# Forty first halves ahead of the expert stage, its first gates loaded in pieces, and a new table of durations for the list scheduler

## The chip, the core and the metric

One NeuronCore of a Trainium2 chip runs the whole program in one launch. The metric is the device time of one execution in microseconds (us), median of the runs given. The engines are TensorE (PE; PEld is its weight load), VectorE (DVE), ScalarE (ACT), GpSimd (POOL) and SyncE (SP). Loads and stores are issued by SP, ACT and POOL and carried by 16 DMA engines.

## The reference, cut to what matters

Two blocks run one after the other on 512 tokens of 1024 channels, in float32: a conformer convolution beside an RWKV-7 recurrence, then a sparse attention, then a convolution and pooling mixer, and at the end a layer of small experts (PEER) and a gated projection. The change is about the expert layer:

```python
def peer_block(xb, w_q, sub_keys, expert_u, expert_v):
    q = (xb @ w_q).reshape(T, 8, 2, 128)
    s = jnp.einsum('thpd,hpkd->thpk', q, sub_keys)       # 128 keys, twice
    sv, si = lax.top_k(s, 16)
    ...                                                   # best 16 of the 16 x 16 sums
    gate = jax.nn.softmax(top_s.astype(jnp.float32), axis=-1)
    u = jnp.take(expert_u, eidx, axis=0)                  # 128 x 128 experts, one row each
    act = jax.nn.gelu(jnp.einsum('thkd,td->thk', u, xb))
    v = jnp.take(expert_v, eidx, axis=0)
    return jnp.einsum('thk,thkd->td', gate * act, v)
```

## The kernel before, in words

The expert layer is done in two ways at once. For 352 of the 512 tokens (TD) it is dense: the 16,384 experts are cut into 128 groups of 128 rows, called experts e below. The first half of e is gelu(U_e x), 24 matmuls of 352 columns; the second half multiplies it by the gates of e, splits it and multiplies it by V_e, 24 more matmuls. Every float32 product is three float32r products of a high and a low part, so each weight tile is split: `wh` on ACT (L207) and `wl` on POOL (L209), in pieces of 256 columns, four for a first half. For the other 160 tokens, rows of U and V are gathered by index (L1338, POOL queue, 512 KB each, 320 of them) and multiplied and summed on DVE (L1353, L1369).

`route` finds the chosen experts and turns them into gates: for each token a one-hot product (L1519 and L1522 on DVE, L1527 on ACT, L1528 on POOL, L1533 on PE, L1536 on ACT) written to `gs` in DRAM by 11 stores of 2 MB, one for 32 tokens (L1537, SP). I call this the one-hot stage. Some first halves need no gate, and NS = 32 of them are done beside `route`: the list `early` takes every fourth e and then, if NS is larger, e = 1, 9, 17 and so on. The gelu of such an expert is stored to `ga` in DRAM (L1208, ACT queue) and loaded back later (L1230, ACT queue). After each one GE gathered rows may be pulled, and after each expert of the last stage GR.

When `route` and the 32 are done, its tile pools close, and the pool `vp` of the last stage opens on the same memory. `prep` runs over experts by threes (GV): for each fourth e it loads the gates of four experts from `gs` into `g4` (L1227, ACT queue, one transfer of 704 KB, two buffers), takes the gelu from `ga` or makes it (`u_phase`, L1199), multiplies it by its gates (L1234), splits it (L241, L242), loads V_e (`vraw`, L1241, SP queue) and splits that too (L1244 on ACT, L1248 on POOL, a quarter at L1246 on DVE). The second halves of three experts follow (L1264 to L1266, sums at L1268). I call this the expert stage.

The order of all instructions on each engine is not that of the program text. `Order` reads the built program, gives every instruction a duration (`cost`), and lists the instructions by a simulation with priorities (`run`); `best` keeps the shortest of twelve such lists, and `impose` makes it the order of each engine. What `cost` and `run` say decides the order of the whole kernel, and only that. `run` also holds each transfer of SP and ACT until the eighth before it has landed (LANES), and the first instruction of a pool until the pools under it are done (`over`).

Of the kernel before, what the change touches and what calls it, by code (L numbers as in the profile page):

```python
# [133 lines left out]
class Net:  # L134
# [1038 lines left out]

    UQ = 1
    NS = 32
    GV = 3
    GA = 4
    BW = 6
# [2 lines left out]
    def peer(self):  # L1182
        nc, tc, I = self.nc, self.tc, self.I
        self.pair.close()
        self.psum2 = None
        with ExitStack() as L:
# [4 lines left out]
            gs = dr.tile([self.TD // 32, 128, 128, 32], F32, name="gs")  # L1191
# [24 lines left out]
            with ExitStack() as VP:  # L1216
                vp = VP.enter_context(tc.tile_pool(name="vp", bufs=1))
                g4 = None
                GV = self.GV

                def prep(e0):
                    nonlocal g4
                    wh, wl, vh, vl = [], [], [], []
                    for e in range(e0, min(128, e0 + GV)):
                        if e % 4 == 0:
                            g4 = vp.tile([128, self.TD // 32, 4, 32], F32, name="g4", bufs=2)
                            nc.scalar.dma_start(g4, gs[:, :, e:e + 4, :].rearrange("g k e t -> k g e t"))  # L1227
                        if e in early:
                            g = up.tile([128, self.TD], F32, name="ga", bufs=self.GA)
                            nc.scalar.dma_start(g, ga[early.index(e)])  # L1230
                        else:
                            g = u_phase(e, False)
                        gv = g.rearrange("p (g t) -> p g t", t=32)
                        nc.vector.tensor_tensor(gv, gv, g4[:, :, e % 4, :], OP.mult)  # L1234
                        h = vp.tile([128, self.TD], F32R, name="wwh", bufs=self.BW)
                        l = vp.tile([128, self.TD], F32R, name="wwl", bufs=self.BW)
                        self.split(h, l, g)
                        wh.append(h)
                        wl.append(l)
                        raw = vp.tile([128, 1024], F32, name="vraw", bufs=2)  # L1240
                        nc.sync.dma_start(raw, I["ev"][e])  # L1241
                        h = vp.tile([128, 1024], F32R, name="vh", bufs=self.BV)
                        l = vp.tile([128, 1024], F32R, name="vl", bufs=self.BV)
                        nc.scalar.activation(h, raw, AF.Copy)  # L1244
                        if e % 8 in self.VD:
                            nc.vector.tensor_tensor(l, raw, h.bitcast(F32), OP.subtract)  # L1246
                        else:
                            nc.gpsimd.tensor_tensor(l, raw, h.bitcast(F32), OP.subtract)  # L1248
                            self.pool = self.last()
                        self.pull(self.GR)  # L1250
                        vh.append(h)
                        vl.append(l)
                    return wh, wl, vh, vl
# [21 lines left out]
    TB = 32  # L1275
    VD = (1, 5)
    GN = 5
    GE = 2.0
    GR = 2.0

    def gather_open(self, L):
# [285 lines left out]
class Order:  # L1567
# [4 lines left out]
    SETS = {"Exp": (0, 6), "Tanh": (0, 2, 18), "Ln": (5, 6), "Silu": (18,), "Sigmoid": (2,), "Sin": (18,),  # L1572
            "Gelu_apprx_tanh": (11,)}
    LOAD, SWITCH, LANES = 1283, 4000, 8
    TICK, BUSY = 10240 / 3, 3060
    SHAPE = 94

    def __init__(self, nc):
# [15 lines left out]
    def cost(self, i):  # L1594
# [3 lines left out]
        out = list(i.outs)  # L1598
# [4 lines left out]
        def psum(a):  # L1603
            return self.mem.get(a.memref, ("",))[0] == "PSUM"
        if "DMA" in op and e == "Pool":
            return e, 0, 1038, 0, 4 * math.prod(c for _, c in out[0].ap)
        if "DMA" in op:
            run = min(list(a.ap)[-1][1] if list(a.ap)[-1][0] == 1 else 1 for a in ins + out)
            return e, 0, 450 if run >= 128 else 625, 0, 4 * math.prod(c for _, c in out[0].ap) * (1 if run >= 128 else 2)
# [3 lines left out]
        if e == "PE":  # L1613
            n = size(out[0])
            rows, cols = i.tile_size
            self.shape[i.name] = rows, cols
            one = n / 2.4
            self.col[i.name] = n * rows / 128
            if i.tile_position[1]:
                return e, cols / 1.2, 20, 20, 0  # L1620
            p = 2 if i.is_transpose else 1 if str(i.ins[0].dtype).endswith("float32r") and n >= 256 else 4
            self.col[i.name] *= p
            return e, cols / (2.4 if i.is_transpose else 1.2), p * one + 2.5, one, 0
        sc = sum(size(a) == 1 for a in ins) if n > 1 else 0
        big = [a for a in ins if size(a) > 1]
        if e == "Activation":
# [2 lines left out]
        if e == "DVE":  # L1629
            if op == "Memset":  # L1630
                return e, 0, n / 0.96 + 8, 0, 0
            fast = op in ("TensorScalarPtr", "TensorCopy") and len(big) < 2 and not any(map(psum, ins))
            return e, 0, (n / (2 if fast else 1) + 66 + 60 * sc) / 0.96, 0, 0
        if op == "Memset":
            return e, 0, n / 1.2 + 36, 0, 0
        return e, 0, n * (2.1 if len(big) > 1 else 3.3) + 150, 0, 0
# [113 lines left out]
    def run(self, pri):  # L1750
# [19 lines left out]
        soon = {e: [] for e in self.HOP}  # L1770
        now = {e: [] for e in self.HOP}
        lanes, cols, ring, dma, array, table, shape = [], {}, 0.0, 0.0, 0.0, None, None
        out = []

        def push(n):
# [12 lines left out]
        while len(out) < len(self.seq):  # L1788
# [31 lines left out]
                lanes.append(dma)  # L1820
            elif e == "PE":
                k = int(max(array, t) / self.TICK)
                slow = 1 if cols.get(k - 1, 0) >= self.BUSY else 2
                d += self.SHAPE if self.shape[n] != shape else 0
                shape = self.shape[n]
                array = end[n] = max(array, t + load * slow) + d * slow
                free[e] = array - last * slow + 3
                k = int(array / self.TICK)
                cols[k] = cols.get(k, 0) + self.col[n]
            else:  # L1830
                end[n] = t + d
                free[e] = end[n] + 3
# [80 lines left out]
```

## Time and profile before

| | us |
|---|---|
| median of 3 runs | 2848.27 (2845.97 to 2852.17) |
| profiled execution, its time | 2844.42 |
| profiled execution, its span | 2842.7 |
| PE busy in the span | 2609.6 |
| DVE busy in the span | 2154.0 |
| POOL busy in the span | 1724.6 |
| ACT busy in the span | 1481.2 |

The span runs from the first to the last instruction of the profiled execution, and all times of the trace are counted from its start. The time of that execution is 1.7 us longer than its span. The mean clock granted to TensorE was 0.965 of full speed.

### The profile page before, as it was taken

How to read it: one execution, taken by the hardware profiler on the slowest of the kernel's cores; microseconds unless marked ns; L12 is line 12 of the kernel's file. 1: busy time of each engine (PE TensorE's matmuls, PEld its weight loads, DVE VectorE, ACT ScalarE, POOL GpSimd, SP SyncE). 2: the span in 40 equal slices, each digit the busy share in tenths (PEclk: the TensorE clock that was granted, in tenths of full speed). 3: DMA queues.
4: the chain of work that ended last, by engine and by line, in shares of the span. 5: the costliest groups of instructions: out<-in, count | busy, mean ns of one | idle time of the engine just before them, and what ended most of it. 6: DMA issues, size and time to landing. Idle time of an engine off the chain costs nothing. (4 is left out here: it accounts for less than half of the span.)

```text
span 2842.7 us, 45654 instructions
## 1 busy us (share of the span) xinstructions
PE 2609.6 (92%) x14715; PEld 2220.0 (78%) x14715; DVE 2154.0 (76%) x4307; ACT 1481.2 (52%) x3177; POOL 1724.6 (61%) x1870
## 2 busy tenths in 40 slices
PE   5889999999798899999999987779999999999996
PEld 3656667666576688887888777779999999999995
DVE  6686669865379998954669999667877787787875
ACT  6646557568455358965353367424334333344435
POOL 4423523222164443346657788779988888899973
PEclk9889899999899999999999999989999999999998
DMA  8744355555872221223334356889999999999972
GB/s 260 172 96 97 82 117 119 103 145 122 216 241 91 71 80 46 71 84 106 92 111 141 107 193 251 293 299 326 338 321 334 334 337 335 309 334 330 336 253 80
DMA packets 353444, 552.27 MB, mean 194 GB/s; under 512 B 60082, under 2 KB 239154, under 8 KB 351539
## 3 DMA queue, kind: packets, MB, share of 16 engines
q1 hardware_dynamic: 224690, 295.22, 32.2%
q0 software_dynamic: 64800, 201.88, 23.9%
q10 hardware_dynamic: 63712, 52.24, 5.8%
q8 instruction: 116, 1.90, 0.3%
q14 instruction: 126, 1.02, 0.1%
HBM read 507.76 MB, written 41.42 MB: 193 GB/s over the span
## 5 line engine op out<-in xcount | busy, mean ns | idle before, releaser
L209 POOL TENSOR_TENSOR wl<-wraw,wh 128x256 fp32r<-128x256 f32 x937 | 748.3, 816 | 395.8 <-ACT wh L207 314.8
L207 ACT ACTIVATE wh<-wraw 128x256 fp32r<-128x256 f32 x937 | 363.0, 411 | 422.0 <-PE mm L217 198.2
L216 PE MATMUL mm<-xh,wh 128*128 128x352 f32 (+1 forms) x1464 | 513.2, 352 | 32.4 <-ACT wh L207 17.4
L218 PE MATMUL mm<-xh,wl 128*128 128x352 f32 (+1 forms) x1464 | 510.6, 352 | 18.8 <-POOL wl L209 18.8
L217 PE MATMUL mm<-xl,wh 128*128 128x352 f32 (+1 forms) x1464 | 510.5, 350 | 2.3 <-DVE xl L287 2.3
L216 PEld LDWEIGHTS mm<-xh,wh 128*128 128x128 f32 x1464 | 280.5, 192 | 57.2 <-ACT wh L207 21.0
L218 PEld LDWEIGHTS mm<-xh,wl 128*128 128x128 f32 x1464 | 280.5, 192 | 42.1 <-POOL wl L209 24.5
L217 PEld LDWEIGHTS mm<-xl,wh 128*128 128x128 f32 x1464 | 280.8, 192 | 23.3 <-DVE xl L287 4.6
L192 POOL DMA_DIRECT2D dl<-in_wev x114 | 100.7, 904 | 284.1 <-ACT dl L191 261.3
L1248 POOL TENSOR_TENSOR vl<-vraw,vh 128x1024 fp32r<-128x1024 f32 x96 | 230.9, 2407 | 4.0 <-ACT vh L1244 3.0
L1369 DVE SCALAR_TENSOR_TENSOR wide<-grow,gdot,wide 128x1024 f32<-128x1024 f32 x158 | 202.4, 1281 | 17.1 <-DMA grow<-in_ev,gidx 15.9
L218 PE MATMUL mm<-xh,dl 128*128 128x512 f32 x456 | 197.0, 436 | 15.5 <-DMA dl<-in_wev 15.5
L1353 DVE SCALAR_TENSOR_TENSOR gscr<-grow,wide 128x1024 bf16<-128x1024 f32 x160 | 194.1, 1213 | 19.4 <-DMA grow<-in_ue,gidx 18.1
L1199 ACT ACTIVATE mm<-mm 128x352 f32<-128x352 f32 x96 | 43.0, 448 | 314.4 <-PE mm L218 308.5
L216 PE MATMUL mm<-xh,dh 128*128 128x512 f32 x456 | 193.4, 428 | 13.0 <-ACT xh L355 12.3
L1338 POOL DMA_INDIRECT grow<-in_ue,gidx x160 | 164.2, 1026 | 57.8 <-DVE gscr L1353 20.2
L217 PE MATMUL mm<-xl,dh 128*128 128x512 f32 x456 | 191.1, 422 | 6.2 <-DVE xl L356 6.2
L1338 POOL DMA_INDIRECT grow<-in_ev,gidx x160 | 162.6, 1016 | 42.8 <-issue 18.1
L1244 ACT ACTIVATE vh<-vraw 128x1024 fp32r<-128x1024 f32 x128 | 134.4, 1054 | 83.2 <-DMA vraw<-in_ev 70.5
L1264 PE MATMUL xu<-wwh,vh 128*128 128x352 f32 x512 | 167.0, 326 | 5.2 <-DVE x L1268 2.6
L1266 PE MATMUL xu<-wwh,vl 128*128 128x352 f32 x512 | 166.1, 326 | 4.6 <-POOL vl L1248 2.6
L1265 PE MATMUL xu<-wwl,vh 128*128 128x352 f32 x512 | 165.8, 324 | 0.0
(582 smaller groups left out, 6818.7 us busy)
## 6 DMA issues: line engine op xcount, KB each, us to landing
vraw<-in_ev SPq DMA_DIRECT2D x128, 512.0 KB, 5.7
wraw<-in_uT SPq DMA_DIRECT2D x494, 128.0 KB, 4.7
draw<-in_wev SPq DMA_DIRECT2D x114, 256.0 KB, 3.4
dl<-in_wev POOLq DMA_DIRECT2D x114, 256.0 KB, 4.7
gs<-st SPq DMA_DIRECT2D x11, 2048.0 KB, 7.7
g<-gs ACTq DMA_DIRECT2D x32, 704.0 KB, 10.3
wraw<-in_wod SPq DMA_DIRECT2D x156, 128.0 KB, 2.2
adaw<-in_adaT SPq DMA_DIRECT2D x32, 512.0 KB, 8.1
```

What stands on the lines that cost most here:

```text
L207: nc.scalar.activation(wh, raw[:, s], AF.Copy)
L209: nc.gpsimd.tensor_tensor(wl, raw[:, s], wh.bitcast(F32), OP.subtract)
L216: nc.tensor.matmul(ps, wh, xh, start=start, stop=False)
L217: nc.tensor.matmul(ps, wh, xl, start=False, stop=False)
L218: nc.tensor.matmul(ps, wl, xh, start=False, stop=stop)
L1248: nc.gpsimd.tensor_tensor(l, raw, h.bitcast(F32), OP.subtract)
L1264: nc.tensor.matmul(po, vh[i][:, s], wh[i], start=(i == 0), stop=False)
L1265: nc.tensor.matmul(po, vh[i][:, s], wl[i], start=False, stop=False)
L1266: nc.tensor.matmul(po, vl[i][:, s], wh[i], start=False, stop=(i == len(wh) - 1))
L1338: self.nc.gpsimd.indirect_dma_start(out=t, out_offset=None, in_=src, in_offset=bass.IndirectOffsetOnAxis(ap=self.gidx[i][:, k:k + 1], axis=0))
L1353: nc.vector.scalar_tensor_tensor(scr, u, 1.0, x, op0=OP.mult, op1=OP.mult, accum_out=self.gdot[i][:, k:k + 1])
L1369: nc.vector.scalar_tensor_tensor(acc, r, w, acc, op0=OP.mult, op1=OP.add)
```

## The change

`NS` goes from 32 to 40, so that the first halves of e = 1, 9, 17, 25, 33, 41, 49 and 57 are done beside `route` too, and `GE` from 2.0 to 1.6, so that the number of gathered rows pulled there stays 64. The first two gate loads (e = 0 and 4) are issued as 11 transfers of 64 KB each. In `Order` the durations of some operations are changed: a float32r matmul costs 12.5 ns more, DVE operations that read two operands from SBUF (or run in the fast mode) cost a quarter more per element, the accumulating transfer of POOL costs less to issue and more to carry, and the clock of PE is followed window by window: it goes up and down at two different counts of columns.

```diff
@@ -1173,7 +1173,7 @@
     UQ = 1
-    NS = 32
+    NS = 40
     GV = 3
@@ -1224,7 +1224,11 @@
                         if e % 4 == 0:
                             g4 = vp.tile([128, self.TD // 32, 4, 32], F32, name="g4", bufs=2)
-                            nc.scalar.dma_start(g4, gs[:, :, e:e + 4, :].rearrange("g k e t -> k g e t"))
+
+                            for i in range(self.TD // 32 if e < 8 else 0):
+                                nc.scalar.dma_start(g4[:, i], gs[i, :, e:e + 4, :])
+                            if e >= 8:
+                                nc.scalar.dma_start(g4, gs[:, :, e:e + 4, :].rearrange("g k e t -> k g e t"))
@@ -1275,7 +1279,7 @@
     GN = 5
-    GE = 2.0
+    GE = 1.6
     GR = 2.0
@@ -1572,7 +1576,8 @@
     LOAD, SWITCH, LANES = 1283, 4000, 8
-    TICK, BUSY = 10240 / 3, 3060
+    TICK, BUSY, FULL = 10240 / 3, 4000, 7200
+    PORT = 1.25
     SHAPE = 94
@@ -1603,7 +1608,8 @@
         if "DMA" in op and e == "Pool":
-            return e, 0, 1038, 0, 4 * math.prod(c for _, c in out[0].ap)
+            add = str(out[0].dtype).endswith("float32r")
+            return e, 0, 920 if add else 1038, 0, (10 if add else 4) * math.prod(c for _, c in out[0].ap)
@@ -1620,7 +1626,7 @@
             self.col[i.name] *= p
-            return e, cols / (2.4 if i.is_transpose else 1.2), p * one + 2.5, one, 0
+            return e, cols / (2.4 if i.is_transpose else 1.2), p * one + (15 if p == 1 else 2.5), one, 0
@@ -1630,7 +1636,8 @@
             fast = op in ("TensorScalarPtr", "TensorCopy") and len(big) < 2 and not any(map(psum, ins))
-            return e, 0, (n / (2 if fast else 1) + 66 + 60 * sc) / 0.96, 0, 0
+            port = fast or sum(not psum(a) for a in big) > 1
+            return e, 0, (n / (2 if fast else 1) * (self.PORT if port else 1) + 66 + 60 * sc) / 0.96, 0, 0
@@ -1770,6 +1777,7 @@
         lanes, cols, ring, dma, array, table, shape = [], {}, 0.0, 0.0, 0.0, None, None
+        tick, slow = 0, 2
@@ -1820,7 +1828,10 @@
                 k = int(max(array, t) / self.TICK)
-                slow = 1 if cols.get(k - 1, 0) >= self.BUSY else 2
+                while tick < k:
+                    c2 = cols.get(tick, 0)
+                    slow = (1 if c2 >= self.FULL / 2 else 2) if slow == 2 else 2 if c2 < self.BUSY else 1
+                    tick += 1
```

## Rows read from the trace of the kernel before

**Rows 1.** Busy time of each engine by stage (window, its length, then each engine).
```profile
core 0: us, PE busy (x) PEld busy (x) DVE busy (x) ACT busy (x) POOL busy (x), PEclk, DMA share, GB/s
0.00:1482.00 1482.00, 1355.82 (x7186) 1019.13 (x7187) 1074.18 (x2151) 891.21 (x1855) 612.38 (x791) 0.96 0.46 120
1482.00:1658.00 176.00, 163.20 (x866) 145.11 (x865) 174.76 (x887) 67.46 (x163) 130.80 (x160) 0.97 0.42 129
1658.00:1806.00 148.00, 117.74 (x866) 108.15 (x864) 144.74 (x136) 114.12 (x305) 122.65 (x90) 0.99 0.63 230
1806.00:1844.00 38.00, 32.21 (x165) 29.90 (x164) 18.86 (x32) 10.31 (x26) 25.75 (x33) 0.87 0.96 347
1844.00:1873.00 29.00, 9.69 (x37) 8.17 (x37) 10.86 (x16) 6.52 (x15) 16.26 (x17) 0.65 0.86 288
1873.00:2760.00 887.00, 870.81 (x5325) 862.31 (x5324) 685.61 (x1029) 349.37 (x742) 791.20 (x757) 0.99 0.95 326
```

**Rows 2.** The same view for single stretches of the expert stage.
```profile
1950.00:2000.00 50.00, 48.96 (x302) 48.20 (x301) 39.10 (x70) 20.21 (x45) 45.81 (x45) 1.00 0.99 345
2200.00:2400.00 200.00, 194.70 (x1189) 191.06 (x1188) 152.16 (x224) 77.73 (x167) 178.08 (x173) 1.00 0.97 335
```

**Rows 3.** Groups of instructions in the one-hot stage, 1658 to 1806 us.
```profile
L1528 POOL TENSOR_TENSOR o<-ob,kt 128x512 f32<-128x512 bf16 x44 | 72.7, 1659 | 16.8 <-DVE ob L1522 16.7
L1519 DVE TENSOR_TENSOR o<-iota,kt 128x1024 f32<-128x1024 f32 x44 | 69.3, 1576 | 0.3 <-PE xu L1533 0.3
L1522 DVE TENSOR_TENSOR ob<-keys,kb 128x1024 bf16<-128x1024 bf16 x44 | 59.5, 1360 | 2.9 <-POOL o L1528 2.9
L209 POOL TENSOR_TENSOR wl<-wraw,wh 128x256 fp32r<-128x256 f32 x26 | 26.6, 1029 | 2.9 <-ACT wh L207 2.8
L1199 ACT ACTIVATE ga<-mm 128x352 f32<-128x352 f32 x7 | 3.2, 456 | 0.8 <-PE mm L218 0.8
```

**Rows 4.** Timeline of ACT, 1806 to 1873 us: start, duration, instruction, idle before it.
```profile
1808.50 0.45 ACT L1199 ACTIVATE ga<-mm 128x352 f32<-128x352 f32 x1
...
1835.63 0.43 ACTq L1227 DMA_DIRECT2D g<-gs  x1
1836.16 5.23 ACTq L1227 DMA_DIRECT2D g<-gs  x1
1846.67 0.46 ACT L1199 ACTIVATE ga<-mm 128x352 f32<-128x352 f32 x1 [4.14 <-issue]
1857.25 0.34 ACTq L1230 DMA_DIRECT2D ga<-ga  x1
1857.64 0.42 ACT L207 ACTIVATE wh<-wraw 128x256 fp32r<-128x256 f32 x1 [10.50 <-DMA g<-gs]
```

**Rows 5.** Timeline of the SP queue around the change of stage.
```profile
1806.86 0.33 SPq L1537 DMA_DIRECT2D gs<-st  x1
1835.63 0.80 SPq L1241 DMA_DIRECT2D vraw<-in_ev  x2
1836.54 22.74 SPq L201 DMA_DIRECT2D wraw<-in_uT  x7
```

**Rows 6.** Timeline of POOL and of PE at the same place.
```profile
1834.86 0.74 POOL L209 TENSOR_TENSOR wl<-wrawx,wh 128x256 fp32r<-128x256 f32 x1
1858.11 0.66 PE L216 MATMUL mm<-xh,wh 128*128 128x352 f32 x1 [14.10 <-ACT wh L207]
```

**Rows 7.** The chain that ended last, at the same place (start, us, what).
```profile
1836.16 21.08 DMA g<-gs
```

**Rows 8.** Waits of the SP queue, 1800 to 1900 us (total, times, longest).
```profile
SPq L201 <- DMA g<-gs: 8.9, 1, 8.9
```

**Rows 9.** Transfers by line, to landing: 1800 to 1880 us, then 1850 to 2720 us.
```profile
g<-gs ACTq DMA_DIRECT2D x2, 704.0 KB, 16.7
g<-gs ACTq DMA_DIRECT2D x30, 704.0 KB, 10.3
```

**Rows 10.** DVE groups of the whole span: gate product and split, gelu from PSUM or from `ga`.
```profile
L1234 DVE TENSOR_TENSOR mm<-mm,g 128x352 f32<-128x352 f32 x96 | 50.8, 529 | 70.3 <-ACT mm L1199 70.1
L242 DVE TENSOR_TENSOR wwl<-mm,wwh 128x352 fp32r<-128x352 f32 x96 | 49.8, 519 | 13.8 <-ACT wwh L241 13.6
L242 DVE TENSOR_TENSOR wwl<-ga,wwh 128x352 fp32r<-128x352 f32 x32 | 34.3, 1071 | 0.3 <-ACT wwh L241 0.3
L1234 DVE TENSOR_TENSOR ga<-ga,g 128x352 f32<-128x352 f32 x32 | 29.8, 932 | 4.3 <-DMA vraw<-in_ev 2.5 <-DMA g<-gs 1.8
```

**Rows 11.** The longest waits of PE, 0 to 1480 us (total, times, longest).
```profile
PE mm L216 <- DMA wraw<-in_wevo: 17.2, 1, 17.2
PE mm L218 <- DMA dl<-in_wev: 15.5, 6, 5.1
```

## The prediction

> **What bounds the kernel now.** I read the busy times by stage first, then the change from the gates' making to the expert stage in the timelines of the engines, then the chain of waits there, then transfers and single operations. The stages have different limits [rows 1]. In the expert stage (1873 to 2760 us) PE is busy 870.8 of 887 us at clock 0.99, and 5325 matmuls in that time are 163.5 ns each; the DMA engines are at 0.95 there, and at 0.97 and 335 GB/s or 0.99 and 345 GB/s in good stretches [rows 2]. So that stage is at PE's limit with DMA just under its own. In the one-hot stage (1658 to 1806 us) DVE is busy 144.7 of 148 us and sets the pace; PE is idle for 30.3 us and POOL for 25.4. Between the two stages lies a hole. From 1806 to 1873 us PE has 25.1 us without work and its granted clock is 0.87 and then 0.65: it ran dry, and then worked partly at the lower of its two levels.
>
> The timelines show how the hole comes about. The last one-hot store is issued at 1806.86 [rows 5]. Seven of the 32 early gelus are still to come then, the first at 1808.50, the last at 1846.67 [rows 4]: 38 us for seven, 5.4 us each, where PE alone needs 24 x 0.1635 = 3.92. The gates could be loaded when the stores have landed, yet the first load is issued at 1835.63 and the first V_e at the same moment on another queue [rows 4, 5]: right behind the last `wl` made from `wrawx` (1834.86 plus 0.74, [rows 6]). What opens the expert stage's memory is thus the end of the early experts, not the stores. Then the second gate load blocks the ACT queue for 5.23 us and lands at 1857.25 [rows 4, 7]; until then ACT sits behind the load of `ga`, and PE waits 14.1 us for `wh` [rows 4, 6].
>
> **The change, part by part.** The sum is made against the profiled execution, 2844.4 us; the median shown is 3.9 us more, and I add that at the end. What a measurement can tell from no change is about 0.2%, 5.7 us.
>
> *Eight first halves leave the expert stage.* They are the e below 64 with e mod 8 = 1. Work it out for eight experts. PE before: eight second halves 8 x 24 x 0.1635 = 31.4 us, six first halves 23.5, together 54.9; sixteen times that is 879 us, and the stage has 887 [rows 1]. After, for e below 64, five first halves: 31.4 + 19.6 = 51.0. DMA for the same eight: eight V_e of 0.524 MB (128 x 1024 floats), five U_e of the same size, two gates of 0.721, three `ga` of 0.180 and 16 gathered rows of 0.524 (GR is 2), 17.2 MB; at 335 GB/s [rows 2] 51.3 us. So DMA takes over as the limit by a hair, and eight experts take 51.3 instead of 54.9 us: 8 x 3.6 = 29 us less. Bounds: 18 us at the stage's mean of 326 GB/s (52.7 us), 31 us if PE stays the limit. I take 29, since 335 is what long stretches show.
>
> The gelus that come from `ga` cost DVE more: the product with the gates 932 instead of 529 ns, the split 1071 instead of 519 [rows 10], 0.96 us for each, 7.6 us for eight. DVE has 201 us idle in the stage [rows 1]; that hides it, as long as DVE stays off the path. Eight more stores and eight more loads of `ga` go through the ACT queue at 0.34 us each [rows 4], 5.4 us of an engine that is idle for 538 of 887 us [rows 1].
>
> *The same eight go in ahead.* There they need PE 8 x 3.92 = 31.4 us and POOL 8 x 4 pieces x 1.03 us [rows 3] = 33 us. The one-hot stage has 30.3 us of PE idle but only 25.4 of POOL [rows 1], in small gaps, so six is the most that can go in and none the least. Before, seven early gelus were made in it [rows 3]. The new table has a say here: it gives the DVE operations of this stage (1024 + 66) / 0.96 = 1135 ns before and (1280 + 66) / 0.96 = 1402 after, where they take 1576 and 1360 [rows 3]. A list that thinks the stage short by 44 x (0.44 + 0.23) = 29 us puts too few early experts between its operations; with the new numbers it is short by 6. I take four inside, free, and four behind at 4.5 us each, between PE's 3.9 and the 5.4 of the stretch (its gathers are shared by more experts, as GE falls): 18 us. Bounds 0 (all fit) and 43 (none, at 5.4).
>
> *The first gates in pieces.* Nothing is removed: 22 transfers of 64 KB for two of 704 KB, all on the ACT queue, and still not before the early experts are done, as above. The hole, 1844 to 1873 us, holds 37 matmuls, 6.0 us at the stage's pace, so 23 us are lost in it. What pieces can do is land as loads of this size land later in the stage, 10.3 us, instead of 21.1 [rows 7, 9], because no issue blocks the queue and other transfers go between. With one first half fewer in the first group (e = 1 is early now), V_e and gates are late next, not U_e. I take 11 us off the hole. Bounds: all 23 off, or 28 on top (first rival).
>
> Behind the pieces on the ACT queue stand the `wh` splits, for which PE waits, so each wait in front of a piece is one of PE too.
>
> *The table elsewhere.* Matmuls of 352 columns go from 149 to 162 ns in the list, against 163.5 traced [rows 1]. All engines get a new order from the first instruction on. In the first 1482 us PE is idle for 126 us, the longest single wait 17.2 us, for a weight [rows 11]. No row says whether a new order takes such a wait away or makes one. I take 0, with one such wait as the bound either way, 17 us.
>
> Sum: -29 + 18 - 11 + 0 = -22 us, 2822 us for a profiled execution, 2826 as a median (-0.8%).
>
> **The rivals.** *The pieces clog the ACT queue (slower).* A load on SP waited 8.9 us for a gate load of the other queue [rows 8], and ACT 10.5 us in front of a `ga` load for the same transfer [rows 4]: transfers wait for earlier ones to land, and the kernel's own list allows eight in flight. 22 pieces are three batches of eight. If each batch lands as late as the two whole loads did, 16.7 us [rows 9], that is 50 us against 21.6 now (1835.63 to 1857.25): 28 us more hole instead of 11 less, -11 + 28 = +17, 2865 us. It decides from about 11 us a batch. Against it: a piece is an eleventh of the bytes, and in front of the expert stage the queues hold less. The Trainium skill, DMA: Bandwidth & Descriptors, section Bandwidth, speaks against this part: it advises 1 MiB a transfer and calls those under 64 KB descriptor-dominated, with 0.95 us for 64 KB and 6.15 us for 1 MB. As an estimate from that page, 22 pieces in a row are 21 us, no sooner than the whole loads now, so the hole would gain nothing and the sum be -11, 2837 us. No row here has a transfer of that shape.
>
> *The extra experts do not fit (no change).* POOL's operations are stretched beside DVE's in the one-hot stage (1029 ns a `wl`), and its gaps are short. Then all eight stand behind it: 8 x 4.5 = 36 us, -29 + 36 - 11 = -4, 2844 us. The part would then only carry the work from one side of the hole to the other. For it: seven of the 32 stand behind it already [rows 4].
>
> *The new order costs more than the gates give (slower).* Two new waits like the longest in the first 1482 us, 34 us, make +12, 2860 us. Against it: the three prices compared with rows above moved towards them. *The new order gives more.* The same wait gone and six experts inside the stage: -29 + 9 - 11 - 17 = -48, about 2800 us.
>
> **How the numbers follow.** The forecast, 2812 to 2842 us, 0.50; more than that, around 2800, 0.18; no change, around 2844, 0.13; the clogged queue 0.10; a costly new order 0.09. That is faster 0.68, same 0.13, slower 0.19. With all good ends it would be -31 + 0 - 23 - 17 = -71, with all bad ones -18 + 43 + 28 + 17 = +70; neither is likely at once. The range 2795 to 2862 leaves out about a third of the larger gain and half of each slower case, 0.15 in all. The likeliest case alone is 2812 to 2842.
>
> **What would show it.** The expert stage has 8 x 24 = 192 matmuls less and is 29 us shorter at a DMA share of 0.97; if its length per expert is unchanged, DMA was its limit. The last one-hot store stays near 1807 us on the stage's own count, with about 11 early gelus behind it; more than that, and the second rival holds. Pieces should land in about 10 us, and PE's wait behind them fall from 14 us to a few; if ACT stands before pieces, the first rival holds. If the stages up to 1482 us move by more than 17 us, the table was the larger half of the change and my zero for it is the step that failed.

## The result, and the profile after

The changed kernel takes 2956.64 us (median of 3 runs, 2955.03 to 2959.93) against 2848.27: 1.0383 times the time before, 95% interval 1.0361 to 1.0405. That is 108 us slower where I had forecast 22 us less. The profiled execution has a span of 2958.2 us.

The page of the profile gives the busy time of each engine (share, instructions), and PE's granted clock in 40 slices of 74 us:

```profile
PE 2655.3 (90%) x14715; PEld 2255.9 (76%) x14715; DVE 2184.5 (74%) x4307; ACT 1490.8 (50%) x3175; POOL 1715.6 (58%) x1870
PEclk9869999896989899999999999979999999999998
```

PE has the same 14,715 matmuls as before, but they take 45.7 us longer, and the clock has dips to 6 in the third and the tenth slice, early in the kernel, where nothing of the expert layer runs. The stages, as in [rows 1] (columns as there):

```profile
0.00:1559.00 1559.00, 1397.84 (x7188) 1048.03 (x7189) 1082.27 (x2143) 885.18 (x1851) 607.48 (x790) 0.92 0.44 114
1559.00:1738.00 179.00, 167.66 (x902) 151.47 (x901) 178.47 (x904) 71.91 (x173) 130.68 (x163) 0.97 0.38 115
1738.00:1933.00 195.00, 165.36 (x1166) 157.84 (x1167) 156.99 (x148) 136.29 (x369) 166.17 (x155) 0.97 0.77 264
1933.00:1972.00 39.00, 9.71 (x60) 9.42 (x58) 22.39 (x38) 7.53 (x17) 25.55 (x27) 0.69 1.03 380
1972.00:2875.00 903.00, 855.40 (x5134) 842.42 (x5134) 699.57 (x1017) 347.25 (x697) 759.69 (x711) 0.98 0.91 314
```

The first stretch, in which the program text is unchanged, holds the same 7187 or so matmuls as before and is 77 us longer, at clock 0.92 instead of 0.96. The one-hot stage is 195 us instead of 148. The hole (one early expert stands behind the last store now, where there were seven) is 39 us instead of the 67 that two rows make up before. The expert stage has 191 matmuls less and is 16 us longer.

In the table below the marks are the same for every kernel, by the line numbers of the kernel before: the last recurrence step (L741), the last step of the top-k (L1484), then the lengths from there to the last gate store (L1537, one-hot), on to the first second half (L1264, hole), and on to the first closing sum (L1397, expert), all of the profiled execution in us; then the median and its ratio to the kernel before on the same chip. e9 and e10 do less work than the others.

| kernel | recurrence end | top-k end | one-hot | hole | expert | median | ratio (95%) |
|---|---|---|---|---|---|---|---|
| before | 724 | 1652 | 155 | 66 | 888 | 2848.27 | |
| changed | 790 | 1732 | 200 | 40 | 903 | 2956.64 | 1.0383 |
| e1 table alone | 774 | 1729 | 155 | 33 | 950 | 2953.88 | 1.0364 (1.0323 to 1.0405) |
| e2 gates alone | 727 | 1653 | 155 | 104 | 876 | 2867.21 | 1.0063 (1.0041 to 1.0084) |
| e3 clock rule alone | 773 | 1690 | 181 | 31 | 913 | 2906.31 | 1.0200 (1.0159 to 1.0241) |
| e4 prices alone | 719 | 1635 | 174 | 27 | 936 | 2852.36 | 1.0017 (0.9997 to 1.0038) |
| e5 old table, other list | 743 | 1657 | 178 | 35 | 929 | 2879.96 | 1.0119 (1.0083 to 1.0156) |
| e6 new table, other list | 776 | 1717 | 156 | 34 | 936 | 2920.08 | 1.0260 (1.0213 to 1.0307) |
| e7 forty ahead, whole gates | 729 | 1662 | 153 | 100 | 870 | 2872.45 | 1.0102 (1.0063 to 1.0140) |
| e8 table from route on | 727 | 1656 | 157 | 34 | 932 | 2858.11 | 1.0031 (1.0008 to 1.0053) |
| e9 no third product | 741 | 1685 | 170 | 50 | 874 | 2869.09 | one execution |
| e10 table, half the rows | 787 | 1744 | 156 | 30 | 907 | 2925.01 | one execution |
| e11 old rule, 4000 | 770 | 1702 | 162 | 55 | 890 | 2890.52 | 1.0147 (1.0094 to 1.0201) |
| e12 two lists joined | 732 | 1645 | 154 | 65 | 893 | 2836.68 | 0.9944 (0.9918 to 0.9969) |
| e13 old prices, never low | 700 | 1613 | 178 | 31 | 917 | 2824.36 | 0.9905 (0.9873 to 0.9937) |
| e14 e8, rows land later | 722 | 1651 | 156 | 27 | 930 | 2856.93 | 1.0030 (1.0000 to 1.0059) |
| e15 old table, rows land later | 731 | 1663 | 156 | 46 | 917 | 2858.88 | 1.0034 (1.0009 to 1.0059) |
| e16 new prices, never low | 697 | 1610 | 156 | 32 | 929 | 2811.84 | 0.9868 (0.9825 to 0.9911) |
| e17 changed, never low | 699 | 1626 | 204 | 40 | 905 | 2840.30 | 0.9972 (0.9950 to 0.9994) |
| e18 changed, old rule | 714 | 1634 | 216 | 31 | 904 | 2866.50 | 1.0072 (1.0051 to 1.0092) |

The 115 us of span divide as 80 up to the end of the top-k (66 of them by the end of the recurrence) and 34 from there to the closing sum (200 + 40 + 903 = 1143 against 1109); the rest lies behind it.

### The profile page after: what moved, and what is told of

The parts are those of the page before. It is cut to its first block, busy times and chain, and to the rows that moved or that the text cites. A ratio compares the mean times of both kernels' runs of the same rounds, so it can differ in the third digit from the quotient of the medians.

```text
span 2958.2 us, 45831 instructions
## 1 busy us (share of the span) xinstructions
PE 2655.3 (90%) x14715; PEld 2255.9 (76%) x14715; DVE 2184.5 (74%) x4307; ACT 1490.8 (50%) x3175; POOL 1715.6 (58%) x1870
## 5 line engine op out<-in xcount | busy, mean ns | idle before, releaser
L207 ACT ACTIVATE wh<-wraw 128x256 fp32r<-128x256 f32 x932 | 374.4, 413 | 607.5 <-PE mm L217 364.9
L216 PE MATMUL mm<-xh,dh 128*128 128x512 f32 x456 | 204.0, 450 | 16.2 <-ACT xh L355 7.0
L217 PE MATMUL mm<-xl,dh 128*128 128x512 f32 x456 | 201.6, 442 | 11.0 <-DVE xl L356 11.0
L1342 POOL DMA_INDIRECT grow<-in_ue,gidx x160 | 171.4, 1071 | 65.0 <-DVE gscr L1357 29.7
L790 DVE SCALAR_TENSOR_TENSOR x<-u,vec,x 128x512 f32<-128x512 f32 x184 | 145.2, 789 | 8.4 <-ACT x L788 5.5
```

Of the source, the lines that this page charges most:

```text
L207: nc.scalar.activation(wh, raw[:, s], AF.Copy)
L216: nc.tensor.matmul(ps, wh, xh, start=start, stop=False)
L217: nc.tensor.matmul(ps, wh, xl, start=False, stop=False)
L1342: self.nc.gpsimd.indirect_dma_start(out=t, out_offset=None, in_=src, in_offset=bass.IndirectOffsetOnAxis(ap=self.gidx[i][:, k:k + 1], axis=0))
```

## The experiments

**Which half? e1 and e2.** e1 has the new table alone, e2 the gates and the forty alone.

```diff
 e1
-    TICK, BUSY = 10240 / 3, 3060
+    TICK, BUSY, FULL = 10240 / 3, 4000, 7200
+    PORT = 1.25
...
 e2
-    NS = 32
+    NS = 40
...
+                            for i in range(self.TD // 32 if e < 8 else 0):
+                                nc.scalar.dma_start(g4[:, i], gs[i, :, e:e + 4, :])
...
-    GE = 2.0
+    GE = 1.6
```

> The new table of durations alone; 32 first halves ahead and whole gate loads, as before. Theory A (the table gives the engines a worse order, above all in the recurrence block up to 790 us, where the changed kernel lost 66 us): slower by about 80 us, 2930 us, with the last recurrence step near 790 us. Theory B (the loss comes from the 40 first halves and the pieces, and the early loss is their knock-on): within 15 us of the kernel before, 2848 us.

> The 40 first halves, GE 1.6 and the pieces alone; the old table. Theory A: the first 1480 us are as before to a few us and the kernel gains what the forecast gave these parts, 2820 to 2845 us. Theory B: the one-hot stage is 33 us longer and the expert stage 15 us longer, as in the changed kernel, 2880 us or more.

e1 alone is 3.6% slower and has the late recurrence (774); e2 is 0.6% slower and has it where it was (727). So the table is nearly the whole loss, and it acts mostly ahead of the layer that the change is about. The gates don't gain either.

**Which number of the table? e3 and e4.** e3 has only the new clock rule (`BUSY`, `FULL` and the loop over `tick`), e4 only the prices of DVE, POOL's transfer and the matmuls.

```diff
 e3
-                slow = 1 if cols.get(k - 1, 0) >= self.BUSY else 2
+                while tick < k:
...
 e4
-            return e, 0, (n / (2 if fast else 1) + 66 + 60 * sc) / 0.96, 0, 0
+            return e, 0, (n / (2 if fast else 1) * (self.PORT if port else 1) + 66 + 60 * sc) / 0.96, 0, 0
...
```

> Of the table only the new model of the PE clock. Theory A1 (the clock model moves the recurrence): last recurrence step near 790 us, 2900 us or more. Theory A2 (the prices of operations move it): last recurrence step near 724 us, 2830 to 2865 us.

> Of the table only the prices (DVE port, accumulating transfer, float32r matmul); the old clock model. Theory A1: last recurrence step near 724 us, 2830 to 2865 us. Theory A2: last recurrence step near 790 us, 2900 us or more. If both e3 and e4 are slow, any change of the list costs, and a list changed by a trifle should too.

The clock rule alone ends the recurrence at 773; the prices alone at 719, and the top-k 17 us sooner than before, which the later stages give back. The two don't add up to e1 (2.0% and 0.2% against 3.6%): e1 has the recurrence of e3, but ends the top-k 38 us later (1729 against 1690). That takes rule and prices together, and no run says why.

**Another list of the same table: e5 and e6.** `best` takes the shortest of twelve lists; here it has to choose among those of one priority weight, so the table is the same and the list another.

```diff
 e5 (old table)
-    def best(self, alphas=(20, 50, 100, 200), rounds=2):
+    def best(self, alphas=(200,), rounds=2):
 e6 (new table)
+    def best(self, alphas=(100,), rounds=2):
```

> A control: the kernel before, its table and all, but only the three lists of alpha 200 to choose from, so that another list of the same old table is imposed. Theory A (the new table, above all its clock model, makes bad lists): another list of the old table stays within 15 us of 2848. Theory C (any other list is slower, the one of before was a lucky one): 2880 us or more.

> The same control for the new table (32 first halves, whole gates): only the lists of alpha 100. Theory A: about as slow as e1, 2920 to 2970 us, with the last recurrence step after 760 us. Theory C: anything between 2850 and 2960 us, and the recurrence may end near 724 us.

Another list of the old table costs 1.2%, 5 us of it by the end of the top-k and 33 behind it: the list of before is a lucky one. Its 888 us of expert stage come back in hardly any other kernel with 32 ahead and all the work (890 in e11, 893 in e12, which takes over the order of before there, 913 to 950 elsewhere). Another list of the new table is 1.0% faster than e1 by the ratios and keeps the late recurrence (776). So, from these two pairs, about 1% is the lot of the list, and 2.6 to 3.6% is more than that.

**Level or memory of the clock rule? e11, e13, e16.** In the list, the old rule calls the clock full if the tick before had at least `BUSY` columns; the new one asks for more and remembers its state. e11 has the old rule with 4000, e13 with 0 (the list never thinks the clock low), e16 the same 0 with the new prices.

```diff
 e11
-    TICK, BUSY = 10240 / 3, 3060
+    TICK, BUSY = 10240 / 3, 4000
 e13, and e16 with e4's prices
+    TICK, BUSY = 10240 / 3, 0
```

> [...] If the higher threshold is what spoils the recurrence block, its last step is near 773 us as in e3. If it is the rule with memory (up at 3600, down at 4000), it is at 720 to 745 us as in the lists of the old rule.

> The old table with the clock never low in the list (threshold 0). [...] If any change of the threshold costs, it is near 760 us.

> The new prices with the clock never low. If a low clock in the list is the harm and the prices are good in the early stages, the mixer ends at 1325 us or earlier (1328 in e4, 1348 before), and the expert stage is as long as with any new prices, 920 to 940 us: 2840 to 2860 us in all.

e11 ends the recurrence at 770, as e3 does (773): the memory shows no cost there, the level does. Over all kernels, whatever their prices and gates: level 4000 (or the new rule) 770 to 790 us, 3060 714 to 743, 0 697 to 700. The windows from the start to that mark (columns as in [rows 1]) of the kernel before, the changed one and e13:

```profile
0.00:724.00 724.00, 643.62 (x4027) 452.97 (x4028) 513.87 (x1142) 448.02 (x942) 253.60 (x370) 0.94 0.57 131
```
```profile
0.00:790.00 790.00, 682.00 (x4006) 479.10 (x4006) 521.41 (x1141) 441.96 (x934) 252.32 (x368) 0.87 0.51 119
```
```profile
0.00:700.00 700.00, 631.42 (x4032) 448.23 (x4033) 512.26 (x1142) 442.75 (x940) 256.19 (x370) 0.96 0.59 136
```

The work is the same: 4006 to 4032 matmuls, 1141 or 1142 DVE operations. Of the changed kernel's 66 us more than before, 38 are PE being busy longer (682.0 against 643.6) at a granted clock of 0.87 instead of 0.94, and 28 are idle (108 against 80). The list that never thinks the clock low gets 0.96 from the chip. The same view of every kernel up to its own mark keeps this order: at level 4000 (or the new rule) the granted clock is 0.86 to 0.90 and PE is idle for 101 to 108 us, at 3060 it is 0.91 to 0.94 and 68 to 87, at 0 0.95 to 0.96 and 58 to 69. e16 came out below what I had expected of it: its expert stage is long, as expected (929), but it ends the top-k at 1610 us, 42 before the kernel before.

**Undoing only the clock rule in the changed kernel: e17 and e18.**

```diff
 e17 (against the changed kernel; e18 has 3060 for 0)
-    TICK, BUSY, FULL = 10240 / 3, 4000, 7200
+    TICK, BUSY = 10240 / 3, 0
-        tick, slow = 0, 2
-                while tick < k:
...
+                slow = 1 if cols.get(k - 1, 0) >= self.BUSY else 2
```

> The changed kernel with one thing other: the clock in the list never low. If the clock model is what made it slow, the recurrence ends at 700 us as in e13 and e16, and the gates cost what they cost alone (18 us in e2): 2830 us, below the kernel before; the whole 126 us faster than the change. If the gates and the prices together were the harm, it stays above 2900 us.

> [...] By stage: the recurrence ends at 720 to 745 us, the mixer near 1330, and the expert layer as in the changed kernel or e2: 2850 to 2875 us, between e17 and the changed kernel. If memory in the rule matters for the expert layer, its one-hot stage is nearer to 155 than to the 200 us of the changed kernel.

With nothing else undone, e17 takes 2840.3 us and e18 2866.5: 116 and 90 us of the changed kernel's time go with the rule. One stretch suggests how. Windows of the changed kernel, then of e17, at about the same place of the recurrence:

```profile
148.00:222.00 74.00, 63.31 (x377) 42.53 (x375) 57.00 (x163) 26.58 (x67) 15.56 (x31) 0.68 0.39 79
```
```profile
140.00:210.00 70.00, 68.79 (x492) 48.20 (x491) 63.92 (x180) 42.46 (x106) 22.60 (x39) 0.98 0.54 108
```

The groups of PE in these two stretches, again the changed kernel first:

```profile
L216 PE MATMUL mm<-xh,dh 128*128 128x512 f32 x33 | 18.4, 558 | 0.0
L626 PE MATMUL tp<-AR,BK 64*128 64x128 f32 x32 | 7.1, 384 | 0.0
L718 PE MATMUL xu<-Xs,Tt 64*64 64x64 f32 x32 | 3.9, 299 | 2.7 <-DVE Xs L714 2.4 <-DVE Ltmp L666 0.3
L711 PE MATMUL xu<-S,AR 64*64 64x64 f32 x28 | 2.8, 292 | 4.2 <-DVE Tp L668 3.3 <-DVE S L738 0.8
```
```profile
L216 PE MATMUL mm<-xh,dh 128*128 128x512 f32 x47 | 19.3, 410 | 0.0
L216 PE MATMUL mm<-uh,pr 128*128 128x512 f32 x12 | 5.0, 414 | 0.0
L626 PE MATMUL tp<-AR,BK 64*128 64x128 f32 x32 | 4.3, 288 | 0.2 <-DVE MT L629 0.2
L718 PE MATMUL xu<-Xs,Tt 64*64 64x64 f32 x32 | 3.0, 242 | 0.0
```

Both hold 32 L626 and 32 L718 of the recurrence. But of the 512-column matmuls of other layers, in threes, the changed kernel puts 3 x 33 = 99 beside them and e17 3 x (47 + 12) = 177. With the thin filling PE is busy 63.3 of 74 us and is granted 0.68; with the thick one it is busy 68.8 of 70 and is granted 0.98. Inside the thin stretch the clock falls after PE had left gaps, stays down in a slice that is full, and is back in the next full one:

```profile
138.00:148.00 10.00, 8.15 (x34) 1.00 0.49 106
148.00:158.00 10.00, 8.84 (x64) 0.88 0.49 94
158.00:168.00 10.00, 10.00 (x64) 0.50 0.50 104
168.00:178.00 10.00, 10.00 (x78) 0.94 0.38 85
```

(Here the columns are PE, clock, DMA share, GB/s.) 0.50 is the lower level, 1.2 GHz. A 512-column matmul then takes 558 instead of 410 ns on the mean of the stretch. I read it so: a list that counts with a low clock believes PE full with half the filling, the order is imposed, and the chip makes it true. That the rule's level sets the loss in the recurrence is shown, and that the granted clock and PE's idle time go with it; what the list believed is argued, from this one stretch. e18's one-hot stage is 216 us and not nearer to 155, so the rule's memory is not what makes that stage long.

**Pieces or forty? e7.** Forty ahead, but all gates in whole loads.

```diff
-    NS = 32
+    NS = 40
-    GE = 2.0
+    GE = 1.6
```

> 40 first halves with GE 1.6, gates loaded whole, old table. If the pieces clog the ACT queue, this is faster than e2 by 15 us or more, 2850 us, and its hole between the last one-hot store and the first second half is shorter than e2's 104 us by as much. If the eight extra first halves behind the one-hot stage are the cause, it is within 6 us of e2, 2867 us, and the hole is 100 us or more.

e2 and e7 have medians of 2867 and 2872 us, on two chips, and ratios of 1.0063 and 1.0102 with intervals that overlap; the hole is 104 us with pieces and 100 without. The pieces do nothing that shows. Transfers in the stretch from 1880 to 1930 us with their median time to landing, e2 and then e7:

```profile
g<-gs ACTq DMA_DIRECT2D x22, 64.0 KB, 8.4
g<-gs ACTq DMA_DIRECT2D x1, 704.0 KB, 8.3
```
```profile
g<-gs ACTq DMA_DIRECT2D x3, 704.0 KB, 14.7
```

A piece of 64 KB needs 8.4 us to land, and the one whole load beside the pieces needs 8.3.

**The table in the expert layer alone: e8, e14, e15.** e8 gives every instruction up to the end of the mixer (`CUT`) the old prices and the old clock rule, and all later ones the new. It still orders the expert stage into 932 us, and DVE waits there for gathered rows; so e14 adds 3.4 us to the landing of a gathered row in the list, and e15 does that with the old table.

```diff
 e8
+        new = int(i.name[2:]) > self.CUT
...
+                if not int(n[2:]) > self.CUT:
+                    slow = 1 if cols.get(k - 1, 0) >= 3060 else 2
 e14 (e8 and this), e15 (before and this)
-                dma = end[n] = max(dma, t + d + 650) + size / 360
+                dma = max(dma, t + d + 650) + size / 360
+                end[n] = dma + (3400 if size == 524288 else 0)
```

> The new prices and clock model only for the expert layer's instructions (route and later); the old ones before it; 32 first halves, whole gates. If the table costs by stage as e1 showed, the first 1462 us stay as before to 5 us, the hole shrinks by 30 us, and the expert stage is 40 to 60 us longer: 2860 to 2880 us. If the long expert stage of e1 came from the earlier stages, it is 888 us as before and the whole 2815 us.

> As e8 (new table from route on), and a gathered row lands 3.4 us later in the list, as traced (6.5 us, where the list has 3.1). If DVE, standing in order in front of rows that have not landed, makes the expert stage long under the new table, that wait (74 us in e8 for both kinds of rows) falls below 40 us and the stage from 932 to 905 us or less. If the wait is only where time is seen and not what sets it, the stage stays at 920 us or more.

> The old table with only that landing time changed. If rows awaited too early are a cost of every list, the expert stage is 870 to 885 us instead of 888 and the whole 2825 to 2845 us. If the list of before was already free of it (27 us of such waits), it is within the spread of lists, 2845 to 2880 us.

e8 is at 1.0031: with the first 1656 us about as before (1652), the new numbers shorten the hole from 66 to 34 us and lengthen the expert stage by 44. e14 was my theory for those 44 us, and it fell. DVE's waits in the expert stage for rows, for a gelu on ACT and for gates, e8 and then e14 (total, times, longest):

```profile
DVE wide L1369 <- DMA grow<-in_ev,gidx: 61.9, 45, 5.1
DVE gscr L1353 <- DMA grow<-in_ue,gidx: 12.3, 11, 2.5
DVE mm L1234 <- ACT mm L1199: 28.5, 18, 5.0
DVE ga L1234 <- DMA g<-gs: 16.8, 7, 6.5
```
```profile
DVE mm L1234 <- ACT mm L1199: 59.6, 38, 4.5
DVE ga L1234 <- DMA g<-gs: 49.1, 18, 6.2
DVE gscr L1353 <- DMA grow<-in_ue,gidx: 30.2, 25, 5.0
DVE wide L1369 <- DMA grow<-in_ev,gidx: 17.5, 19, 2.8
```

Those for rows fall from 74.2 to 47.7 us, and the stage goes from 932 to 930. The two others grow by 31 and 32 us: DVE waits for something else instead, and the wait for rows by itself did not set the length. With the old table (e15) the later landing gains nothing either: 1.0034, within the spread of lists.

**What limits the expert stage? e9 and e10.** e9 is the kernel before without the third product of every second half; e10 is e1 with every second gathered row left out (and half as many pulled after each expert).

```diff
 e9
-                            nc.tensor.matmul(po, vh[i][:, s], wl[i], start=False, stop=False)
-                            nc.tensor.matmul(po, vl[i][:, s], wh[i], start=False, stop=(i == len(wh) - 1))
+                            nc.tensor.matmul(po, vh[i][:, s], wl[i], start=False, stop=(i == len(wh) - 1))
 e10
-            for k in range(n):
+            for k in range(0, n, 2):
...
```

> The kernel before without the third product of the second halves (the V_e low part times the high part of the gated gelu): 1024 matmuls less, 167 us of PE; every transfer stays. If PE sets the length of the expert stage, it falls from 888 to about 725 us and the whole to 2690. If the DMA engines or the gathered rows set it, it stays above 830 us.

> The new table as in e1, with every second gathered row left out: 160 of 320 rows, half of their transfers and of their DVE and POOL work. If the rows and their transfers make the expert stage long under the new lists (950 us in e1), it falls to PE's own 870 to 885 us. If the order of PE, ACT and POOL makes it long, it stays above 920 us.

The expert stage of e9 (window, then what PE waits for longest in it) and of e10 (window):

```profile
1906.00:2780.00 874.00, 752.53 (x4242) 709.15 (x4241) 679.64 (x980) 339.05 (x719) 767.16 (x720) 0.96 0.92 315
```
```profile
PE mm L218 <- POOL wl L209: 64.4, 66, 3.4
```
```profile
1930.00:2838.00 908.00, 874.21 (x5322) 864.76 (x5323) 527.60 (x829) 365.04 (x736) 659.49 (x611) 0.99 0.74 239
```

With 118 us less of PE the stage is 14 us shorter, and PE then waits for the splits of POOL, which has its gathers between them and is busy 767 of 874 us. With half the rows POOL and DMA have room (0.74), the stage is 950 - 907 = 43 us shorter than in e1, and PE is busy for 874 of 908. The 907 us lie between the two outcomes I had named, and the 43 us are hardly more than the 41 by which two lists of the old table differ in this stage (888 and 929). e9 is the firmer of the two, though of one execution: PE had 871 us of work, and with 118 of them gone POOL, the rows and DMA (share 0.92) still hold the stage at 874. So two limits lie close together, which of POOL and DMA makes the second no run separates, and PE's share alone doesn't price a saving.

**Two lists joined: e12.** Up to the mixer the order of e4 (prices new, rule old), behind it that of before, merged by planned starts.

```diff
+class Priced(Order):
+    NEW = True
...
+    key = {n: new.at[n] if int(n[2:]) <= Order.CUT else old.at[n] + d for n in old.seq}
```

> Two lists joined at the end of the mixer: up to there the list made by the new prices with the old clock rule (e4, 20 us earlier at that place), behind it the list of the kernel before. If stages keep their length with their list, the mixer ends near 1330 us and the rest takes 1495 us as before: 2825 us, faster by 0.7%. If the length of a late stage hangs on more than its own order, the 20 us are given back: 2840 to 2860 us.

2836.7 us, 0.9944: 7 us of top-k end gained (1645), not the 17 of e4's own list, while the lucky rest of before is kept at 1112 instead of 1109. e16 is better.

## Why the prediction was wrong, point by point

**The step that failed is "The table elsewhere", priced at 0 with 17 us either way.** Measured in its place: +66 us by the end of the recurrence and +80 by the end of the top-k, over four times my bound. I looked in the diff at the prices, which moved towards rows, and in the trace at single waits [rows 11]; the clock rule I did not weigh at all. With it the list packs PE less densely in the recurrence, and the chip's clock follows (0.94 before, 0.87 after, 0.96 in e13). Undone in the changed kernel, it gives back 91 us by that mark (699 in e17). The rival with a costly new order had the right sign and stage, but a wrong mechanism (two waits, 34 us) and too small a chance, 0.09. My own sentence for this case holds: the stages up to 1482 us moved by 77 us, so the table was the larger half.

**Expert stage, -29.** Measured for the forty, each against the kernel of the same table and rule with 32: -12 (e2), -18 (e7), -24 (e17 against e16), -32 (e18 against e4). My bounds were 18 to 31: the size was about right, and the scatter of the lists wider. PE's busy time falls by 34 us between e16 and e17, as worked out (31.4 by 192 matmuls); the length by less, as PE isn't the only limit (e9); nor did DMA take over, at a share of 0.91 and not 0.97. In the changed kernel the stage is even 15 us longer than before, because 888 was a lucky order: against e1, the same table with 32, it is 47 us shorter.

**The same eight ahead, +18, bounds 0 to 43.** Too low. With the old table one of the eight fits (8 early gelus in the one-hot stage, 7 before), and 14 or 15 stand behind the last store, not 11: the hole takes them, +38 (e2) and +34 (e7), so the rival that the experts don't fit was right in mechanism and near in price (36); what it set against that, -29, was the smaller part. With the new prices the lists do the opposite (the changed kernel, e17, e18) and put 20 early gelus into the one-hot stage, which then lasts 200 us instead of 155. It is not the prices alone: with 32 ahead, lists of the old prices put up to 13 there too (e5 and e13, 178 us). I had said that at most six more fit, for want of POOL; 13 more went in. The groups of POOL and of DVE in that stage of the changed kernel, 1732 to 1933 us, beside [rows 3]:

```profile
L209 POOL TENSOR_TENSOR wl<-wraw,wh 128x256 fp32r<-128x256 f32 x70 | 62.2, 902 | 9.3 <-ACT wh L207 8.8
L1532 POOL TENSOR_TENSOR o<-ob,kt 128x512 f32<-128x512 bf16 x44 | 54.4, 1241 | 6.1 <-PE xu L1537 3.6 <-DVE ob L1526 1.7 <-PE tp L1537 0.7
L1342 POOL DMA_INDIRECT grow<-in_ue,gidx x34 | 47.6, 1400 | 15.7 <-DVE gscr L1357 8.0 <-PE tp L1537 2.5 <-issue 2.3
```
```profile
L1523 DVE TENSOR_TENSOR o<-iota,kt 128x1024 f32<-128x1024 f32 x44 | 86.1, 1958 | 1.2 <-PE xu L1537 1.0
L1526 DVE TENSOR_TENSOR ob<-keys,kb 128x1024 bf16<-128x1024 bf16 x44 | 41.6, 948 | 20.0 <-POOL o L1532 17.5 <-ACT st L1540 1.6 <-ACT ga L1199 0.9
L1357 DVE SCALAR_TENSOR_TENSOR gscr<-grow,wide 128x1024 bf16<-128x1024 f32 x30 | 36.4, 1212 | 16.8 <-DMA grow<-in_ue,gidx 16.6
```

Before, POOL waited 16.7 us for DVE's `ob` and DVE 2.9 for POOL's `o` [rows 3]; now DVE waits 17.5 us for `o` and POOL 1.7 for `ob`: POOL is ahead no longer, with 70 pieces of `wl` where it had 26, busy for 166 of 195 us. DVE's own two operations cost 127.7 us together, as before (69.3 + 59.5 = 128.8 [rows 3]); but it waits another 16.6 us for rows, and multiplies 30 rows there at 1.2 us. What my price left out were those rows: each early expert pulls GE of them, 34 gathers are issued in the stage, and they need POOL and DVE in the very stage that has neither. They are not the reason in every list: e18 also has 20 early gelus there, issues 18 rows and has the longest stage, 216 us. Its list makes the 20 first, with DVE waiting for 81.2 us in one piece, and the one-hot products after. Price of the forty in one-hot stage and hole: 48 + 8 = 56 us (e17 against e16). So the part that my sum did price fails in its sign as well: eight first halves and pieces cost 18 us in e2 by its ratio, and 28 us in the median from e16 to e17 (2811.8 and 2840.3), where I had -22.

**Pieces, -11, bounds -23 to +28.** Measured: nothing (e7 against e2). The first rival, the clogged queue, is there in kind, since ACT does stand in front of pieces, but not in price, since it stood so in front of a whole load. ACT in the hole of the changed kernel (start, duration, idle before), then what PE waits for first, then the landing of the pieces from 1940 to 2000 us:

```profile
1949.39 8.49 ACTq L1229 DMA_DIRECT2D g<-gs  x6
1957.93 1.06 ACT L1248 ACTIVATE vh<-vraw 128x1024 fp32r<-128x1024 f32 x1 [14.73 <-DMA g<-gs]
1957.95 4.51 ACTq L1229 DMA_DIRECT2D g<-gs  x5
1962.51 1.06 ACT L1248 ACTIVATE vh<-vraw 128x1024 fp32r<-128x1024 f32 x1 [3.52 <-DMA g<-gs]
1970.97 1.06 ACT L1248 ACTIVATE vh<-vraw 128x1024 fp32r<-128x1024 f32 x1 [6.48 <-DMA vraw<-in_ev]
1971.93 0.48 ACT L241 ACTIVATE wwh<-ga 128x352 fp32r<-128x352 f32 x1
```
```profile
1972.46 0.66 PE L1268 MATMUL xu<-wwh,vh 128*128 128x352 f32 x1 [29.75 <-ACT wwh L241]
```
```profile
g<-gs ACTq DMA_DIRECT2D x22, 64.0 KB, 7.2
```

The queue blocks behind pieces as it did behind one whole load, 8.5 and 4.5 us for 5.23 [rows 4], and ACT's split of V_e stands behind it. Each piece lands in 7.2 us, sooner than the 10 that I gave it, and it helps nothing: PE waits 29.75 us. What comes last before its first product is the third V_e, for which ACT waits another 6.48 us; that V_e and gates are late next was in my forecast. The short hole of this kernel comes from having one early expert behind the last store instead of seven: it is 104 and 100 us with 14 and 15 of them (e2, e7), 66 with seven, 40 with one. The estimate from the Trainium skill, DMA: Bandwidth & Descriptors, section Bandwidth, had the pieces gain nothing, and the runs agree. That section's 0.95 us for 64 KB is the engines' busy span for transfers issued from GpSimd; a piece, issued from ACT, took 7.2 to 8.4 us here to its landing, with the DMA engines at a share of about 1.

**What opens the expert stage's memory.** I said the early experts and not the stores. That is how I read the order of before. In the changed kernel the last store is issued at 1932.79 and the first V_e at 1945.15, and the trace puts the last 2.4 us of wait in front of it down to transfers of `ga`; what opened the memory there is not settled.

**The range** of 2795 to 2862 would have held e17 (2840), which is the change without its clock rule, and not the change. That would have been luck: there the forty cost 28 us, and what brings e17 below the kernel before are the new prices with a clock that is never low.

The best kernel found is e16: the new prices, a list that never counts with a low clock, 32 ahead and whole gates: 2811.8 us, 0.9868 of before, interval 0.9825 to 0.9911; e13, with the old prices, overlaps it (0.9873 to 0.9937). What stays open is why the expert stage of before is so short (888 where e4, e8 and e16 have 929 to 936): the three prices were only changed together, and the landing time that I changed by itself (e15, 917) doesn't explain it.

## What to carry to other kernels

A table that feeds a list scheduler is judged by the order that it makes, not by how near its numbers are to the trace: run each number by itself, and beside it another list of the same table, to know how much is chance (here 1%). A planner that counts with a throttled clock can bring it about: look at the granted clock of unchanged stages before pricing anything else. Before a saving is priced at an engine's pace, take work away from that engine (e9) and see whether the stage gets shorter; and work moved into a stage with a free engine also brings the work that hangs on it (here gathered rows for POOL and DVE).

## What the runs showed of the hardware

The same 4000 or so matmuls took 631 us of PE time at a mean granted clock of 0.96 (e13) and 682 at 0.87 (the changed kernel), by order alone. DVE operations with both operands in SBUF stretch further than the new table thinks, on the mean. It gives 352 columns (352 x 1.25 + 66) / 0.96 = 527 ns; the split of a `ga` took this in the changed kernel (whole span):

```profile
L242 DVE TENSOR_TENSOR wwl<-ga,wwh 128x352 fp32r<-128x352 f32 x40 | 48.3, 1216 | 0.7 <-ACT wwh L241 0.7
```

That is 1216 ns, against 519 for the same split with one operand in PSUM [rows 10]. The trace also shows when it stretches. Of these 40 splits 15 overlap no TENSOR_TENSOR of POOL and take 517 ns on the mean, near the table's 527; the other 25 take 1636. With one operand in PSUM the split takes 519 ns in either case. An example: DVE, then POOL, in the same few us of the changed kernel.

```profile
1969.73 0.95 DVE L1238 TENSOR_TENSOR ga<-ga,g 128x352 f32<-128x352 f32 x2
1972.60 2.69 DVE L242 TENSOR_TENSOR wwl<-ga,wwh 128x352 fp32r<-128x352 f32 x2
```
```profile
1969.49 0.94 POOL L1342 DMA_INDIRECT grow<-in_ue,gidx  x1 [0.30 <-issue]
1972.10 2.37 POOL L1252 TENSOR_TENSOR vl<-vraw,vh 128x1024 fp32r<-128x1024 f32 x1 [0.41 <-ACT vh L1248]
```

Two products in 0.95 us beside the issue of a gather, two splits in 2.69 beside a split of POOL. The Trainium skill, SBUF — State Buffer, section Who interferes with whom, has a DVE instruction with two SBUF inputs contend with a GpSimd instruction that reads SBUF; the trace agrees with it.
